# A one-core encoder block: small tiles are widened or added in three pools, so that the tiles behind them begin at multiples of 64 bytes

## The chip, the cores and the metric

The kernel runs on one core of a Trainium2 chip. The metric is the device time of one execution in microseconds (us). Three executions of the kernel before took 2293.75, 2299.6 and 2301.99 us; the median is 2299.6 us.

## The reference

One encoder layer on 2048 positions with 1024 channels, all in float32. Half of the mixer's channels go through a two-dimensional Fourier transform, the other half through a gated long convolution (Hyena) whose filters come from a small network. A squared-ReLU MLP of width 4096 follows.

```python
h   = rmsnorm(x, g_mix);  p = h @ w_in                  # 1024 -> 2048
y_f = rmsnorm(fourier_mix(p[..., :512]), g_fourier)     # Re(FFT2), 8 groups x 64 channels
y_h = rmsnorm(hyena_mix(p[..., 512:], ...), g_hyena)    # z = gate * (fft_long_conv(z, k) + d z), twice
x   = x + concat(y_f, y_h) @ w_out
a   = square(relu(rmsnorm(x, g_mlp) @ w_fc1))           # 1024 -> 4096
x   = x + a @ w_fc2                                     # 4096 -> 1024
out = rmsnorm(x, g_final)
```

## The kernel before

**Two kinds of matmul.** Where float32 accuracy is wanted at speed, an operand is split into a high and a low part of type float32r (`split`, lines 184 to 188: ScalarE casts the high part, VectorE or GpSimd subtracts it for the low part), and `mm3` (lines 198 to 200) issues three matmuls: high by high, high by low, low by high. The transforms use plain float32 matmuls instead, and the trace has two records for each of those. In a matmul the stationary operand is loaded into the array first (LDWEIGHTS) and the moving operand, up to 512 columns, streams past it. A row of the profile such as `p1u<-zf,ahm` names the result, then the moving operand, then the stationary one.

**Stages, in order of time.** `project` (0 to about 410 us) computes `p` in two passes. `filters` (to about 615 us) generates eight spectra: `generate` makes the time-domain filter in two halves `kh` and `kl` (for two of the eight units in one tile `k`), `stage1` multiplies them with the constant table `e1h`, `e1l` by `mm3` in groups of three, `stage2` is plain float32 with the table `f2`. `fourier` runs beside it. `hyena` (to about 840 us) is plain float32: `first` reads `zz`, `second` the table `f2h`, `inverse` the table `a2`, which lies in the tile of `f2`. `project_out` (to about 1040 us) is `mm3` again, then `fc1` (to about 1672 us) and `fc2` (to the end), both with Strassen-like products m1 to m7.

**The MLP's first half.** `fc1` makes 32 steps. A step has seven products (`fc1_product`), each twelve matmuls on one row of 512 tokens: four slices by `mm3`. The moving operands are token tiles that stay: m1 and m2 lie in `zf`, a tile of 32 KB per partition (line 1000); m3, m5, m6 and m7 lie in the tiles `G` and `V` (rows `bm`), m4 in `bhm` and `blm`. The stationary operands are weight slices `ahm` and `alm`, split anew in each step. The order on TensorE within a step is m1 (`p1u<-zf`), m4 of the step before (`p1u<-bhm`), m2 (`p1m<-zf`), m3 of the step before (`p1v<-bm`), m6, m5, m7. After step 15 the token tiles are loaded anew for the second half of the tokens. The last lines of `fc1` make another `zf` in the same place, which holds both operands of the first products of `fc2` (rows `p2u<-zf` and `p2m<-zf`).

**Where a tile lies.** A pool lays its tiles one behind the other in each partition of the on-chip memory, from a left or from a right end; tiles take multiples of 32 bytes. Pools with side "right" (`cp0`, `zp`, `tabs`, `ep`, `norms`, `gk`, `spectra`, `fourier`) are stacked from the high end downwards, and that end lies 32 bytes off a multiple of 64 in this kernel. `uf`, `zz`, `k` (two units) and `zf` are one buffer of `zp` after another. In the built program the tiles that the text speaks of begin at these offsets behind a multiple of 64 bytes:

| tile | before | after | used as |
|---|---|---|---|
| `zf` (fc1) | 32 | 0 | moving, float32r, against `ahm`, `alm` at 0 |
| `zf` (first products of fc2) | 32 | 0 | moving and stationary, float32r |
| `kh`, `kl`, `k` | 32 | 0 | moving, float32r, against `e1h`, `e1l` at 0 |
| `bm`, `bhm`, `blm`, `G`, `V`, `wh`, `xh`, `qah`, `qbh` | 0 | 0 | float32r, both sides |
| `f2`, `f2h`, `emb`, `e1z`, `b1` | 32 | 0 | stationary, float32 |
| `zz`, `uf`, `wo`, `hid`, `feat` | 32 | 0 | moving, float32 |
| `y` | 0 | 0 | moving, float32, against `a2` in the tile of `f2` |
| `ident`, `xt`, `hm` | 0 | 0 | transposes |
| `e1f`, `ones`, `turn` (the table) | 32 | 32 | small constants |

Of the kernel before, what the change touches and what calls it, by code (L numbers as in the profile page):

```python
# [10 lines left out]
F32 = mybir.dt.float32  # L11
# [118 lines left out]
P = 128  # L130
# [6 lines left out]
def hybrid_block(ctx: ExitStack, tc: tile.TileContext, A, out):  # L137
    nc = tc.nc
# [26 lines left out]
    def pool(name, side="left"):  # L165
        return tc.tile_pool(name=name, bufs=1, side=side, reuse_waits="tile")

    def pa(nm):
        return ps.tile([P, 512], F32, tag="a", name=nm, bufs=8)

    def load(pl, tag, shape, src, bufs=1):
        t = pl.tile(shape, F32, tag=tag, name=tag, bufs=bufs)
        nc.sync.dma_start(t, src)
        return t
# [89 lines left out]
    def filter_hidden(fh):  # L264

        yield
        with tc.high_priority(offset=120):
            w0 = load(fh, "w0", [66, P], A["filt_w0"])
            wi = load(fh, "wi", [P, 2, P], A["filt_wi"])
            fb = load(fh, "fb", [P, 4], A["filt_bf"])  # L270
            first = load(fh, "feat", [66, 512], A["feat"][:, 0:512], 2)
        for half in range(2):
            cur = {}
            for layer in range(3):
                for q in (2 * half, 2 * half + 1):
                    if layer == 0:
                        cur[q] = load(fh, "feat", [66, 512], A["feat"][:, 512 * q : 512 * q + 512], 2) if q else first
                    p = pa(f"ph{layer}")
                    nc.tensor.matmul(p, lhsT=w0 if layer == 0 else wi[:, layer - 1, :], rhs=cur[q], start=True, stop=True)
                    a = fh.tile([P, 512], F32, tag="arg", name="arg", bufs=2)  # L280
                    nc.vector.tensor_scalar(out=a, in0=p, scalar1=fb[:, layer : layer + 1], scalar2=fb[:, 3:4], op0=ALU.add, op1=ALU.mult)
                    n = fh.tile([P, 512], F32, tag="turn", name="turn")
                    nc.vector.tensor_scalar(out=n, in0=a, scalar1=1.0 / TAU, scalar2=MAGIC, op0=ALU.mult, op1=ALU.add)
                    nc.vector.tensor_scalar(out=n, in0=n, scalar1=MAGIC, scalar2=None, op0=ALU.subtract)
                    for c in TAU_PARTS:
                        nc.vector.scalar_tensor_tensor(out=a, in0=n, scalar=-c, in1=a, op0=ALU.mult, op1=ALU.add)
                    nc.vector.tensor_scalar(out=a, in0=a, scalar1=PI_IN, scalar2=-PI_IN, op0=ALU.min, op1=ALU.max)
                    if layer < 2:
                        cur[q] = fh.tile([P, 512], F32, tag="hid", name="hid", bufs=2)
                        nc.scalar.activation(cur[q], a, AF.Sin)  # L290
                        yield
                        continue
                    emb = fh.tile([P, 8, P], F32, tag="emb", name="emb", bufs=2)
                    nc.gpsimd.memset(emb, 0.0)
                    for h in (slice(0, 64), slice(64, 128)):
                        nc.scalar.activation(emb[h, :, h], a[h].rearrange("h (l p) -> h l p", l=8), AF.Sin)
                    if q == 0:

                        nc.vector.tensor_copy(emb[64:128, 0, 0:1], emb[0:64, 0, 0:1])
                    nc.sync.dma_start(embd[:, 8 * q : 8 * q + 8, :], emb)  # L300
                    yield
# [207 lines left out]
    def filters(ctx, tp, fx, fp, gp, zp, zzs, norms, emb, wo, e1k, f2, dk8, tabs):  # L509
# [2 lines left out]
        e1h, e1l = (fp.tile([P, P], FR, tag=n, name=n) for n in ("e1h", "e1l"))  # L512
        split(e1h, e1l, e1k)

        longd = fp.tile([P, 8], F32, tag="longd", name="longd")
        p = pa("plongd")
        nc.tensor.transpose(p[:, 0:8], dk8, ident[0:8, 0:8])
        nc.scalar.copy(longd, p[:, 0:8])
# [840 lines left out]
    def run(*steps):  # L1359

        live = list(steps)
        while live:
            live = [g for g in live if next(g, live) is not live]
# [4 lines left out]
    with pool("ip") as ip, pool("cp1") as cp1:  # L1368
        with pool("cp0", "right") as cp0:
            run(project(ip, fx, (cp0, cp1), (1, 2), None), filter_hidden(cp0), fourier_weights(cp0))  # L1370
        zstack, tabs, early = (ctx.enter_context(ExitStack()) for _ in range(3))
        zp = zstack.enter_context(pool("zp", "right"))
        uf = zp.tile([P, NT, 512], F32, tag="zz", name="uf")
        tp = tabs.enter_context(pool("tabs", "right"))
        ep = early.enter_context(pool("ep", "right"))
        got, ffs = [], []

        w2 = A["w_fc2"].rearrange("(h f p) d -> p h f d", h=2, p=P)

        def second_weights(room, tiles):  # L1380


            rows = A["w_fc2"].rearrange("(h f p) d -> p h f d", h=2, p=P)
            room = room.rearrange("p f c -> p (f c)").rearrange("p (n h d) -> p n h d", n=2, h=2)
            for f, tile_f in enumerate(tiles):
                t = room[:, f % 2]
                nc.scalar.copy(t[:, 0, 0:1], uf[:, tile_f, 0:1])
                nc.sync.dma_start(t, rows[:, :, f, :])
                b11, b12, b21, b22 = (t[:, h, 512 * e : 512 * e + 512] for h in range(2) for e in range(2))
                nc.vector.tensor_sub(b11, b12, b11)  # L1390
                nc.vector.tensor_sub(b12, b22, b12)
                nc.vector.tensor_sub(b22, b22, b11)
                nc.vector.tensor_sub(b21, b21, b22)
                nc.sync.dma_start(td[:, f], t.rearrange("p h (e d) -> p (h e) d", e=2))
                yield

        def tables():
            yield
            yield
            got.extend(load(cpool, n, [P, P], A[n]) for n in ("e1f", "e1k", "turn"))  # L1400
            got.append(load(cpool, "gy", [P, 8], A["g_y"]))
            got.append(cpool.tile([8, 128], F32, tag="dk8", name="dk8"))
            for n in range(2):
                nc.sync.dma_start(got[-1][4 * n : 4 * n + 4, :], A["long_d"].rearrange("a (c n) j -> n (a c) j", n=2)[n])
            f2, emb = (pl.tile([P, 32, P], F32, tag=n, name=n) for pl, n in ((tp, "f2"), (tp, "emb")))

            second = second_weights(f2, [15, 0, 0, 1, 2, 3, 4, 5, 6, 7, 8, 9, 10, 11, 12, 13])
            got.append(load(tp, "e1z", [P, 2, P], A["e1z"]))
            got.append(load(ep, "wo", [P, 2, 512], A["filt_wo"]))
            got.extend((emb, f2))  # L1410
            for f in range(0, 32, 8):
                next(second)
                yield
                if f in (0, 8):
                    next(second)
                nc.sync.dma_start(emb[:, f : f + 8], embd[:, f : f + 8])

            for f in (1, 5, 9, 11, 13, 15):
                next(second)
                yield  # L1420
                if f == 1:
                    next(second)
                n = 4 if f < 9 else 2
                t = fx.tile([P, n, 2, P], F32, tag="xt" if n > 2 else "st", name="ff", bufs=6 - n)
                nc.sync.dma_start(t, A["ff"][:, f : f + n])
                ffs.extend(t[:, j : j + 2] for j in range(0, n, 2))
            for _ in second:
                yield
            for f in range(0, 32, 8):
                nc.sync.dma_start(f2[:, f : f + 8], A["f2k"][:, f : f + 8])  # L1430

        run(project(ip, fx, (None, cp1), (-1, 0), uf), tables())
        e1f, e1k, turn, gy, dk8, e1z, wo, emb, f2 = got
    norms = early.enter_context(pool("norms", "right")).tile([P, 4, 128], F32, tag="norms", name="norms")
    with pool("filters") as fp:
        zzs, f2h = [], []
        gp = early.enter_context(pool("gk", "right"))
        spx = early.enter_context(ExitStack())
        filt = filters(spx, tp, fx, fp, gp, zp, zzs, norms, emb, wo, e1k, f2, dk8, f2h)
        with pool("fourier", "right") as fo:  # L1440
            ffs.insert(0, load(fo, "ff0", [P, 1, 2, P], A["ff"][:, 0:1]))
            for i, _ in enumerate(fourier(fo, uf, e1f, ffs)):
                if i % 2 == 0 and i < 16 or 16 <= i < 24:
                    next(filt)
        run(filt)
# [73 lines left out]
```

## Time and profile before

| | |
|---|---|
| three executions | 2293.75, 2299.6, 2301.99 us |
| profiled execution, first to last instruction | 2296.7 us |
| TensorE busy | 2238.5 us, 97% |
| VectorE, ScalarE, GpSimd busy | 65%, 48%, 36% |
| mean granted TensorE clock | 0.991 |
| DMA | 487.31 MB, 212 GB/s over the span |

The profile gives the span of the profiled execution and no separate time for it; the span is 2.9 us under the median of the three executions and within their spread. "Busy" of TensorE counts records whose ends are modelled: matmuls are pipelined, one record of 512 columns lasts 390 ns while the next begins after about 227 ns. So this text reads the distance from start to start in the timeline view (start, length, engine, line, operation, names, shape, count; in brackets idle time before it and what ended that). In the windows view a row has the stretch, its length, and for each engine its busy time and number of records, then the granted clock, the DMA share and GB/s. In the views of one tile or one line, a row has the number of records, the shortest, median and longest duration in ns, and the first and last start.

### The profile page before, as it was taken

Reading aid. Unit: us, or ns where it says so; the run is one execution under the profiler, and the core shown is the slowest. Engines: PE = TensorE matmul, PEld = TensorE weight load, DVE = VectorE, ACT = ScalarE, POOL = GpSimd, SP = SyncE. Lnnn points to the kernel's source line nnn. Section 1 sums busy time; section 2 is a strip of 40 time slices with the busy share of each in tenths; the row PEclk is TensorE's granted clock in tenths of the full one; section 3 lists DMA queues with packets and bytes.
Section 4 is the critical chain, followed back from the end, with each engine's and each line's share of the span. In section 5 each row is a group of like instructions: output and inputs, shape, how many; then the busy total and the mean of one; then the engine's idle time right before and its main releaser. Section 6 shows DMA issues by size and latency. Waiting matters only on the chain.

```text
span 2296.7 us, 31041 instructions
## 1 busy us (share of the span) xinstructions
PE 2238.5 (97%) x11025; PEld 1855.9 (81%) x11025; DVE 1501.3 (65%) x2254; ACT 1108.8 (48%) x1849; POOL 826.0 (36%) x627
## 2 busy tenths in 40 slices
PE   8999999999999989998999989999999999999998
PEld 6887788799788858886888878888888888888886
DVE  6999676777578774458444465444477666866667
ACT  6555211566366564455555565555543333533333
POOL 3444323576476611146555546555400000000000
PEclk9999999999999999999999999999999999999999
DMA  8535886689987766667444475444489766866631
GB/s 270 184 133 198 315 304 247 223 289 324 337 264 210 214 194 188 180 197 234 156 149 150 151 247 164 152 152 151 143 316 344 246 189 196 297 197 194 192 119 74
DMA packets 298798, 487.31 MB, mean 212 GB/s; under 512 B 17478, under 2 KB 141712, under 8 KB 294418
## 3 DMA queue, kind: packets, MB, share of 16 engines
q1 hardware_dynamic: 292977, 470.91, 62.2%
q10 hardware_dynamic: 5664, 14.41, 1.8%
q8 instruction: 87, 1.43, 0.3%
q14 instruction: 70, 0.57, 0.1%
HBM read 314.64 MB, written 169.05 MB: 211 GB/s over the span
## 4 chain that ended last, share of the span: by engine, by line
PE 85%; DVE 5%; DMA 4%; ACT 3%; issue 2%; POOL 1%; SPq 0%; ACTq 0%; DVEq 0%; POOLq 0%
PE p2u L198 5%; PE p2u L199 5%; PE p2u L200 5%; PE p1u L198 5%; PE p1u L200 5%; PE p1u L199 5%; PE pu L200 4%; PE pu L199 4%; PE pu L198 4%; PE p2v L198 3%; PE p2v L199 3%; PE p2v L200 3%; PE pk L610 2%; PE p1v L198 2%; PE p1v L200 2%; PE pz L729 2%
## 5 line engine op out<-in xcount | busy, mean ns | idle before, releaser
L184 ACT CAST qahm<-ra 128x1024 fp32r<-128x1024 f32 x110 | 115.9, 1053 | 345.2 <-PE p2u L199 172.0
L185 DVE TENSOR_TENSOR qalm<-ra,qahm 128x1024 fp32r<-128x1024 f32 x110 | 134.7, 1225 | 153.7 <-ACT qahm L184 151.8
L1293 POOL TENSOR_TENSOR acc<-acc,gfin 128x512 f32<-128x512 f32 x4 | 5.1, 1278 | 631.9 <-DMA out<-acc 624.7
L198 PE MATMUL pu<-wh,xh 128*128 128x512 f32 x512 | 204.3, 400 | 5.6 <-ACT wh L187 4.4
L199 PE MATMUL pu<-wl,xh 128*128 128x512 f32 x512 | 201.7, 394 | 3.7 <-DVE wl L188 3.6
L200 PE MATMUL pu<-wh,xl 128*128 128x512 f32 x512 | 201.6, 394 | 1.2 <-DVE xl L185 1.2
L199 PE MATMUL p2u<-qblm,qahm 128*128 128x512 f32 x504 | 196.3, 390 | 0.0
L198 PE MATMUL p2u<-qbhm,qahm 128*128 128x512 f32 x504 | 196.1, 390 | 0.0
L200 PE MATMUL p2u<-qbhm,qalm 128*128 128x512 f32 x504 | 196.0, 390 | 0.0
L185 DVE TENSOR_TENSOR qblm<-rb,qbhm 128x1024 fp32r<-128x1024 f32 x110 | 134.1, 1219 | 2.6 <-ACT qbhm L184 2.4
L393 POOL TENSOR_TENSOR acc<-acc,cw 128x512 f32<-128x512 f32 x45 | 59.9, 1332 | 196.8 <-DVE acc L370 193.5
L184 ACT CAST ahm<-s 128x512 fp32r<-128x512 f32 x124 | 76.7, 621 | 100.9 <-PE p1v L199 55.3
L185 POOL TENSOR_TENSOR alm<-W,ahm 128x512 fp32r<-128x512 f32 x63 | 86.2, 1369 | 97.8 <-ACT ahm L184 97.8
L198 PEld LDWEIGHTS pu<-wh,xh 128*128 128x128 f32 x512 | 97.2, 190 | 26.3 <-ACT wh L187 4.8
L199 PEld LDWEIGHTS pu<-wl,xh 128*128 128x128 f32 x512 | 97.3, 190 | 25.3 <-DVE wl L188 4.9
L184 ACT CAST qbhm<-rb 128x1024 fp32r<-128x1024 f32 x110 | 115.3, 1048 | 4.7 <-DMA rb<-in_w_fc 3.4
L200 PEld LDWEIGHTS pu<-wh,xl 128*128 128x128 f32 x512 | 97.2, 190 | 22.8 <-DVE xl L185 2.8
L198 PEld LDWEIGHTS p2u<-qbhm,qahm 128*128 128x128 f32 x504 | 94.7, 188 | 20.0 <-issue 0.3
L200 PEld LDWEIGHTS p2u<-qbhm,qalm 128*128 128x128 f32 x504 | 94.7, 188 | 19.6
L199 PEld LDWEIGHTS p2u<-qblm,qahm 128*128 128x128 f32 x504 | 94.7, 188 | 19.5
L198 PE MATMUL p1u<-bm,ahm 128*128 128x512 f32 x252 | 100.3, 398 | 9.4 <-ACT ku L1155 9.4
L184 ACT CAST ahm<-W 128x512 fp32r<-128x512 f32 x94 | 57.5, 615 | 101.5 <-PE p1u L199 101.5
(397 smaller groups left out, 6428.6 us busy)
## 6 DMA issues: line engine op xcount, KB each, us to landing
W<-in_w_fc SPq DMA_DIRECT2D x66, 512.0 KB, 4.6
spec<-ks SPq DMA_DIRECT2D x32, 1024.0 KB, 6.2
ks<-spec SPq DMA_DIRECT2D x64, 512.0 KB, 4.9
rb<-td SPq DMA_DIRECT2D x64, 512.0 KB, 4.1
ra<-a1m SPq DMA_DIRECT2D x56, 512.0 KB, 3.9
ra<-a0m SPq DMA_DIRECT2D x54, 512.0 KB, 5.8
rb<-in_w_fc SPq DMA_DIRECT2D x46, 512.0 KB, 4.9
f<-in_w_fc SPq DMA_DIRECT2D x16, 1024.0 KB, 8.2
```

What stands on the lines that cost most here:

```text
L184: nc.scalar.copy(hi, src)
L185: (eng or nc.vector).tensor_sub(lo, src, hi)
L198: nc.tensor.matmul(o, lhsT=lh, rhs=rh, start=start, stop=False, skip_group_check=more)
L199: nc.tensor.matmul(o, lhsT=lh, rhs=rl, start=False, stop=False, skip_group_check=more)
L200: nc.tensor.matmul(o, lhsT=ll, rhs=rh, start=False, stop=stop, skip_group_check=more)
L393: nc.gpsimd.tensor_add(m1, m1, cw[:, 3, :])
L610: nc.tensor.matmul(p[:, 128 * j : 128 * j + 128], lhsT=f2[:, 4 * q + j, :], rhs=self.G[:, :, 4 * q + j], start=True, stop=True)
L729: nc.tensor.matmul(p[:, 256 * sp : 256 * sp + 256], lhsT=e1[:, sp, :], rhs=zz[:, :, lo : lo + 16], start=True, stop=True)
L1293: nc.gpsimd.tensor_mul(acc[i][:, c], acc[i][:, c], gfin[:, c])
```

## The change

In the pool `cp0` the bias tile `fb` is declared 16 columns wide, of which four are used, and a tile `edge` of 32 bytes is added at the pool's end. In the pool `filters` the tile `longd` is declared 16 columns wide, of which eight are used. In the pool `zp` a tile `edge` of 32 bytes is added beside the large buffer. Nothing reads or writes the added columns or the two `edge` tiles. Each engine gets the same instructions in the same order as before, and TensorE and the DMA queue of SyncE wait for the same events; three instructions elsewhere lose a wait for an earlier DMA, and two such waits of ScalarE move from one instruction (`neg`) to one thirteen instructions later (`sb`). What differs is where tiles lie, by 32 bytes in either direction.

```diff
         with tc.high_priority(offset=120):
             w0 = load(fh, "w0", [66, P], A["filt_w0"])
             wi = load(fh, "wi", [P, 2, P], A["filt_wi"])
-            fb = load(fh, "fb", [P, 4], A["filt_bf"])
+            fb = fh.tile([P, 16], F32, tag="fb", name="fb")[:, 0:4]
+            nc.sync.dma_start(fb, A["filt_bf"])
             first = load(fh, "feat", [66, 512], A["feat"][:, 0:512], 2)
...
-        longd = fp.tile([P, 8], F32, tag="longd", name="longd")
+        longd = fp.tile([P, 16], F32, tag="longd", name="longd")[:, 0:8]
...
             run(project(ip, fx, (cp0, cp1), (1, 2), None), filter_hidden(cp0), fourier_weights(cp0))
+            cp0.tile([P, 8], F32, tag="edge", name="edge")
         zstack, tabs, early = (ctx.enter_context(ExitStack()) for _ in range(3))
         zp = zstack.enter_context(pool("zp", "right"))
         uf = zp.tile([P, NT, 512], F32, tag="zz", name="uf")
+        zp.tile([P, 8], F32, tag="edge", name="edge")
```

## The prediction

> **What bounds the kernel now.** First the head of the page, then the windows view over the stages that the change can reach.
>
> ```profile
> span 2296.7 us, 31041 instructions
> PE 85%; DVE 5%; DMA 4%; ACT 3%; issue 2%; POOL 1%; SPq 0%; ACTq 0%; DVEq 0%; POOLq 0%
> 460.00:575.00 115.00, 115.00 (x870) 106.09 (x869) 88.16 (x158) 72.52 (x147) 81.40 (x69) 1.00 0.87 308
> 1040.00:1080.00 40.00, 35.03 (x149) 28.15 (x150) 31.16 (x32) 26.81 (x45) 24.41 (x15) 0.91 0.80 261
> 1083.00:1351.00 268.00, 268.00 (x1170) 219.41 (x1169) 122.61 (x141) 148.55 (x252) 156.44 (x112) 1.00 0.49 162
> 1378.00:1672.00 294.00, 294.00 (x1271) 240.46 (x1271) 138.51 (x159) 160.64 (x270) 159.94 (x114) 0.99 0.47 152
> 1690.00:2270.00 580.00, 580.00 (x2560) 480.45 (x2559) 404.44 (x491) 231.19 (x252) 0.00 (x0) 1.00 0.66 218
> ```
>
> TensorE holds 85% of the chain that ended last. After the stretch and its length, a window row has TensorE's matmuls, its weight loads, VectorE, ScalarE, GpSimd, granted clock, DMA share and GB/s. In the filters (460 to 575 us), in `fc1` (1083 to 1351 and 1378 to 1672) and in `fc2` TensorE is busy in all of the stretch at a granted clock of 0.99 to 1.00. No other engine passes 77% there, and in `fc1` none passes 60%. So a nanosecond less per matmul in these stretches is a nanosecond less in the span, and the other engines keep up. Only at the start of `fc1` (1040 to 1080) TensorE waits: 35 of 40 us.
>
> Busy time doesn't show whether those matmuls run at full speed. The timeline of one step of `fc1` does. Each row is the first matmul of a run of twelve; the column to read is the start.
>
> ```profile
> 1332.17 0.39 PE L198 MATMUL p1u<-bm,ahm 128*128 128x512 f32 x1
> ...
> 1334.89 0.40 PE L198 MATMUL p1u<-zf,ahm 128*128 128x512 f32 x1
> ...
> 1337.69 0.40 PE L198 MATMUL p1u<-bhm,ahm 128*128 128x512 f32 x1
> ...
> 1340.45 0.40 PE L198 MATMUL p1m<-zf,ahm 128*128 128x512 f32 x1
> ...
> 1343.25 0.40 PE L198 MATMUL p1v<-bm,ahm 128*128 128x512 f32 x1
> ...
> 1346.01 0.39 PE L198 MATMUL p1u<-bm,ahm 128*128 128x512 f32 x1
> ...
> 1348.73 0.39 PE L198 MATMUL p1v<-bm,ahm 128*128 128x512 f32 x1
> ```
>
> Twelve matmuls on `bm` take 2.72 us (1332.17 to 1334.89, and again 1346.01 to 1348.73), which is 227 ns each. Twelve on `zf` take 2.80 us, both times: 233 ns each. And the run behind each `zf` run, though its tile is at offset 0, takes 2.76 us: something that the `zf` run has left behind is worked off there. So a `zf` run costs 0.08 + 0.04 = **0.12 us** more than one on an aligned tile.
>
> Is that the offset? Two more sets of rows bear on it: those of one tile (shortest, median and longest duration in ns, first and last start), and a stretch of the timeline at the start of `fc2`.
>
> ```profile
> L198 PE MATMUL p1u<-zf,ahm x120: 393/397/400, 1080.0 to 1654.9; 128*128 128x512 f32 x120
> L198 PE MATMUL p1v<-bm,ahm x252: 388/390/629, 1068.8 to 1677.8; 128*128 128x512 f32 x126
> L198 PE MATMUL p2m<-zf x8: 389/390/390, 1683.0 to 1687.8; 128*128 128x512 f32 x8
> L198 PE MATMUL pk<-kh,e1h x48: 392/397/496, 456.8 to 604.9; 128*128 128x512 f32 x48
> 1680.55 0.39 PE L199 MATMUL p2u<-zf 128*128 128x512 f32 x1
> ...
> 1683.27 0.39 PE L199 MATMUL p2m<-zf 128*128 128x512 f32 x1
> ```
>
> The median is 397 ns where the moving operand stands at 32 and the stationary one at 0: for `zf` against `ahm`, and also for `kh` against `e1h`, other tiles in another stage. It is 390 ns where both stand at 0 (`bm`), and also where both stand at 32 (`p2m<-zf`): twelve of those take 2.72 us, from 1680.55 to 1683.27. So offset 32 alone costs nothing in a row of like matmuls; a moving operand at 32 beside a stationary one at 0 does. The change sets both to 0, a pair that the trace shows at full speed.
>
> **Part by part: `zf` in `fc1`.** 32 steps with two `zf` runs are 64 runs. The four runs of the first two steps lie between 1040 and 1080 us, where TensorE waits for others anyway; I count them as nothing. The other 60 save 60 x 0.12 = **7.2 us**. Two waits stand in the middle, where the token tiles are loaded anew:
>
> ```profile
> 1354.10 0.50 PE L198 MATMUL p1u<-bm,ahm 128*128 128x512 f32 x1 [2.02 <-ACT ku L1155]
> 1377.59 0.79 PE L198 MATMUL p1u<-bm,ahm 128*128 128x512 f32 x1 [3.82 <-ACT ku L1155]
> 1378.18 0.63 PE L199 MATMUL p1u<-bm,ahm 128*128 128x512 f32 x1
> ...
> 1382.87 0.63 PE L199 MATMUL p1u<-zf,ahm 128*128 128x512 f32 x1
> ```
>
> The loads and splits behind them start from TensorE's last use of the old tiles, which comes earlier by what was saved until then, so they keep that saving; within a step TensorE arrives up to 0.24 us sooner, so at most some 0.2 us are given back at each. After the longer wait eleven matmuls take 4.69 us (1378.18 to 1382.87), 426 ns each instead of 227: the array runs at half its rate for that long. [...] I take nothing for it; twelve matmuls at 0.2 us more, 2.4 us, are a bound upwards, well inside the range below.
>
> **`kh`, `kl`, `k` in the filters.** 192 matmuls stand at 32 against 0, but in short runs between plain float32 work. What does an aligned run look like there? `project_out` shows one behind transposes:
>
> ```profile
> 482.02 0.40 PE L199 MATMUL pk<-k,e1h 128*128 128x512 f32 x1
> ...
> 483.19 0.38 PE L542 MATMUL pk<-wo,emb 128*128 128x128 f32 x2
> 562.48 0.40 PE L199 MATMUL pk<-kl,e1h 128*128 128x512 f32 x1
> ...
> 567.85 0.83 PE L542 MATMUL pk<-wo,emb 128*128 128x128 f32 x6
> 899.81 0.40 PE L199 MATMUL po<-G,oyh 128*128 128x512 f32 x1
> ...
> 900.97 0.39 PE L198 MATMUL po<-V,oyh 128*128 128x512 f32 x1
> ...
> 902.35 0.39 PE L198 MATMUL po<-G,oyh 128*128 128x512 f32 x1
> ```
>
> Counted from the second matmul, a run of six takes 1.17 us in the filters (482.02 to 483.19) and its first five take 1.16 us in `project_out` (899.81 to 900.97): aligned runs start slowly too, so a short one gains 0.01 us, and one of twelve not much more. A run of 24 takes 5.37 us (562.48 to 567.85) against 2.54 us for eleven aligned (899.81 to 902.35) and 12 x 0.227 = 2.72 us for the rest, 5.26 us: 0.11 us. There are two runs of 24 and 19 shorter ones: 0.22 + 19 x 0.015 = **0.5 us**.
>
> **The plain float32 matmuls.** The tables `f2`, `f2h`, `a2` and `emb` come from 32 to 0, in 4 x 512 = 2048 records.
>
> ```profile
> L752 PE MATMUL pv<-y,f x512: 270/275/579, 633.1 to 820.3; 128*128 128x128 f32 x171
> L542 PE MATMUL pk<-wo,emb x512: 270/275/418, 408.3 to 583.5; 128*128 128x128 f32 x171
> L610 PE MATMUL pk<-Gk,f x512: 269/273/379, 466.6 to 613.7; 128*128 128x128 f32 x171
> L736 PE MATMUL pz<-G,f2h x512: 270/273/422, 621.7 to 812.0; 128*128 128x128 f32 x171
> L233 PE MATMUL pt_m<-ident,hm x128: 272/273/330, 860.7 to 1047.4; 128*128 128x128 f32 x128
> ```
>
> With the stationary table at 32, the moving operand at 0 (`y`) and at 32 (`wo`) have the same median, 275 ns: here the pair's offsets don't matter. The trace has no such matmul with both at 0; the nearest are the transposes, at 273 ns. So between a gain of 2 ns and, by the same distance the other way, a loss of 2 ns: 2048 x 2 = 4.1 us either side. I take 0, by the two equal rows. The wider tiles, the `edge` tiles and the five moved waits add no work to any engine.
>
> **Sum.** 7.2 + 0.5 = 7.7 us off a span of 2296.7 us gives 2289.0 us. The median of the executions is 2.9 us over that span, so 2299.6 - 7.7 = **2291.9 us**, -0.33%. A measurement of this kernel can tell about 0.5% (11.5 us) from no change, so the forecast lies inside that.
>
> **Rivals.** (1) *The change does nothing*: 2299.6 us. Offset 32 is not what slows the `zf` runs; it is something else about their place. For it: `p2m<-zf` in the same bytes runs at 390 ns. Against it: `kh` shows the same 397 ns elsewhere, and the pair of offsets tells all these rows apart. [...] (2) *The float32 matmuls gain too*: 2291.9 - 4.1 = 2287.8 us, if both operands at 0 give what the transposes show. (3) *The other side: float32 matmuls with both at 0 get slower*, because moving and stationary reads that start alike collide. From 7.7 us / 2048 = 3.8 ns a record on the gain is gone; at the 7 ns that `zf` shows (397 against 390) they would cost 14.3 us: 2299.6 + 6.6 = 2306.2 us. Against it: float32r pairs at 0 and 0 are the fastest rows there are, and the rows of lines 542 and 752 do not react to the moving operand's offset.
>
> **How the numbers follow.** Forecast 72%, rival 1 15%, rival 2 8%, rival 3 5%. The three executions before spread over 8 us, so a median of a few can be 3 us off. The range goes from rival 2's 2287.8 less 3 to rival 1's 2299.6 and half a microsecond: 2285 to 2300, which leaves out rival 3 and the noisy half of rival 1. Faster by over 0.5% needs 2288.1 or less: most of rival 2 and a tenth of the forecast, 0.15. Slower by over 0.5% needs 2311: 0.03, rival 3 at a higher price. Within: 0.82.
>
> **What the changed profile would show.** Right: the `zf` rows at a median of 390 ns, 2.72 us from run to run through the whole step, a step of `fc1` of 84 x 0.2267 = 19.04 us instead of 19.28; `pk<-kh` runs of 24 at 5.26 us; lines 542, 610, 736 and 752 at 273 to 275 ns. Rival 1: `zf` stays at 397. Rivals 2 and 3: lines 542 and 752 move. Wrong altogether: the waits before 1354 and 1377 us grow by what was saved.

## Result and profile after

Five executions of the kernel after took 2286.55 to 2289.84 us, median **2289.36 us**. Five of the kernel before have a median of 2298.18 us. The ratio is 0.9963, with a 95% interval of 0.9952 to 0.9974: faster by 0.4%, 8.8 us.

The head of the page:

```profile
span 2288.0 us, 31038 instructions
PE 2229.5 (97%) x11025; PEld 1854.2 (81%) x11025; DVE 1503.7 (66%) x2254; ACT 1109.5 (48%) x1849; POOL 827.4 (36%) x627
```

Two rows of the windows view (stretch, length, then TensorE, weight loads, VectorE, ScalarE and GpSimd, granted clock, DMA share, GB/s):

```profile
460.00:575.00 115.00, 115.00 (x870) 106.36 (x869) 88.87 (x159) 72.21 (x146) 82.26 (x69) 1.00 0.87 307
1690.00:2270.00 580.00, 580.00 (x2559) 479.73 (x2558) 405.27 (x502) 230.44 (x253) 0.00 (x0) 1.00 0.64 215
```

The span is 8.7 us shorter, and TensorE is as busy as before, 97% of the span and all of these stretches, at the same clock. The shares alone show no change. The timeline of a step of `fc1` does (first matmul of each run of twelve; the column to read is the start):

```profile
1327.89 0.39 PE L198 MATMUL p1u<-bm,ahm 128*128 128x512 f32 x1
...
1330.61 0.39 PE L198 MATMUL p1u<-zf,ahm 128*128 128x512 f32 x1
...
1333.33 0.39 PE L198 MATMUL p1u<-bhm,ahm 128*128 128x512 f32 x1
...
1336.05 0.39 PE L198 MATMUL p1m<-zf,ahm 128*128 128x512 f32 x1
...
1338.77 0.39 PE L198 MATMUL p1v<-bm,ahm 128*128 128x512 f32 x1
```

Every run now takes 2.72 us, whichever tile moves. The runs on `zf` took 2.80 us before, and the runs behind them 2.76 us. How much that adds up to is read from the rows of one tile: `p1m<-zf` of `fc1`, before and then after (shortest, median and longest duration in ns, first and last start).

```profile
L198 PE MATMUL p1m<-zf,ahm x120: 394/397/400, 1089.8 to 1660.4; 128*128 128x512 f32 x120
```

```profile
L198 PE MATMUL p1m<-zf,ahm x120: 389/389/389, 1088.5 to 1651.9; 128*128 128x512 f32 x120
L198 PE MATMUL pk<-kh,e1h x48: 387/394/501, 457.6 to 605.1; 128*128 128x512 f32 x48
L737 PE MATMUL pz<-G,f2h x512: 270/272/421, 621.9 to 811.2; 128*128 128x128 f32 x171
L753 PE MATMUL pv<-y,f x512: 270/275/550, 633.8 to 820.3; 128*128 128x128 f32 x171
L543 PE MATMUL pk<-wo,emb x512: 269/275/422, 407.5 to 583.7; 128*128 128x128 f32 x171
```

The kernel after is 1.3 us ahead at the first of these matmuls (1089.8 against 1088.5) and 8.5 us ahead at the last (1660.4 against 1651.9). So `fc1` gave 7.2 us of the 8.7. In the filters the first `kh` matmul starts 0.8 us later than before and the last 0.2 us later: 0.6 us were won there. The rows of plain float32 stand where they stood: 275 ns for lines 543 and 753, 272 instead of 273 for line 737. What is left, about 0.9 us, came from waits elsewhere: by the start times the kernel after loses 0.8 us ahead of the filters, gains 1.5 us between the filters and `fc1`, and 0.2 us behind it. Such waits differ from execution to execution: the eight kernels below that are the same as the kernel after up to `fc1` reach their first `kh` matmul anywhere between 455.6 and 461.5 us.

### The profile page after: what moved, and what is told of

Same layout as the page of the kernel before. It is cut to its first block, busy times and chain, and to the rows that moved or that the text cites. A ratio compares the mean times of both kernels' runs of the same rounds, so it can differ in the third digit from the quotient of the medians.

```text
span 2288.0 us, 31038 instructions
## 1 busy us (share of the span) xinstructions
PE 2229.5 (97%) x11025; PEld 1854.2 (81%) x11025; DVE 1503.7 (66%) x2254; ACT 1109.5 (48%) x1849; POOL 827.4 (36%) x627
## 4 chain that ended last, share of the span: by engine, by line
PE 81%; DVE 3%; DMA 2%; ACT 2%; issue 1%; POOL 1%; SPq 0%; ACTq 0%; POOLq 0%; DVEq 0%
PE p2u L198 5%; PE p2u L199 5%; PE p2u L200 5%; PE p1u L200 5%; PE p1u L198 5%; PE p1u L199 5%; PE p2v L198 3%; PE p2v L199 3%; PE p2v L200 3%; PE pv L753 2%; PE pu L200 2%; PE pu L199 2%; PE pu L198 2%; PE pk L611 2%; PE p1v L200 2%; PE p1v L199 2%
```

## Experiments

The expectations name their theories themselves; theory A is the reason that the prediction gives, that the pair of offsets modulo 64 decides. All diffs are against the kernel after, unless the text says otherwise. A median of several executions comes with a ratio and its interval; where there is one execution, no ratio is given.

**One line of the change alone.** Of the whole change only the `edge` tile of the pool `zp` is kept:

```diff
         uf = zp.tile([P, NT, 512], F32, tag="zz", name="uf")
+        zp.tile([P, 8], F32, tag="edge", name="edge")
```

> Only the 32-byte tile in the pool of zf is added; kh and kl of four units stay at 32, and so does what lies in cp0. Theory A (a matmul is slow where its moving and its stationary row begin at different offsets mod 64) and theory B (a moving row that begins at 32 is slow, whatever the stationary one does): zf rows go to 389 ns, fc1 gains the 7.4 us that it gained with the whole change, the filters some 0.2 us; 0.9966 of before, 2290 to 2291 us. Theory C (the place of zf or the shift of the left pools does it, not the offset mod 64): no more than half of that.

Measured: 2289.8 us, ratio 0.9963 (0.9950 to 0.9975), the same as the whole change.

```profile
L198 PE MATMUL p1m<-zf,ahm x120: 389/389/389, 1088.3 to 1651.3; 128*128 128x512 f32 x120
L198 PE MATMUL pk<-kh,e1h x48: 389/397/483, 456.7 to 604.0; 128*128 128x512 f32 x48
```

`zf` is at 389 ns, and from its first to its last row here `fc1` takes 563.0 us, where the kernel before takes 570.6: 7.6 us. So the place of `zf` is nearly the whole gain, and the other three edits can't be seen in the total. The line moves more than `zf`, though: all pools stacked behind `zp` on the right side shift with it, and so `k` and some `kh` tiles come to their new place too. The `kh` rows stay at 397 in the median, with the tiles of the left pool still in their old place.

**The filters' line alone.** Only `longd` is widened:

```diff
-        longd = fp.tile([P, 8], F32, tag="longd", name="longd")
+        longd = fp.tile([P, 16], F32, tag="longd", name="longd")[:, 0:8]
```

> Only longd is widened: kh and kl of three or four units in the left pool come to 0, zf stays at 32. Theories A and B: zf rows stay at 397 ns, fc1 as before; runs of kh in the filters lose 0.01 us each, the one run of 24 that is moved 0.1 us; the time is that of before within 0.5 us of its usual scatter. Theory C: part of the gain of fc1 shows here.

Measured: 2297.61 us in one execution, beside a median of 2297.3 for the kernel before. Twelve matmuls on `zf` still take 2.80 us, and the twelve behind them 2.76:

```profile
1296.13 0.40 PE L198 MATMUL p1u<-zf,ahm 128*128 128x512 f32 x1
...
1298.93 0.40 PE L198 MATMUL p1u<-bhm,ahm 128*128 128x512 f32 x1
...
1301.69 0.40 PE L198 MATMUL p1m<-zf,ahm 128*128 128x512 f32 x1
```

**Is it the place of `zf`, or the pair?** The weight rows `ahm`, `alm` are moved 32 bytes on (m1 and m2 of the first two steps, and m5 and m6 of the first, take their weights from another pool and stay):

```diff
+        mp.tile([P, 8], F32, tag="pad0", name="pad0")
         for h in "hl":
             mp.tile([P, 4, P], FR, tag=f"a{h}", name=f"a{h}", bufs=9)
+        mp.tile([P, 8], F32, tag="pad1", name="pad1")
```

> The kernel after, with the stationary weights of fc1 moved to 32 by a 32-byte tile in front of them (steps 2 to 31; another behind them keeps the rest in place). Every pair in fc1 is then 0 against 32. Theory A: all 84 matmuls of a step are slow, 233 to 237 ns each instead of 227, a step takes 19.6 to 19.9 us instead of 19.04, and the kernel 2306 to 2315 us. Theories B and C: nothing moves, 2289 us, since no moving row has changed.

Measured: 2305.93 us, ratio 1.0037 (1.0026 to 1.0048). Slower than the kernel *before*: now every run takes 2.80 us, though `zf`, `G` and `V` lie where the kernel after has them (`bhm` and `blm` begin 64 bytes further on).

```profile
1300.55 0.40 PE L198 MATMUL p1u<-zf,ahm 128*128 128x512 f32 x1
...
1303.35 0.40 PE L198 MATMUL p1u<-bhm,ahm 128*128 128x512 f32 x1
...
1320.14 0.40 PE L198 MATMUL p1u<-zf,ahm 128*128 128x512 f32 x1
```

A step takes 19.6 us (1300.55 to 1320.14) instead of 19.04, and the total is at the low end of what theory A expected. So it is no property of the moving tile alone. The next kernel also takes the `edge` tile of `zp` away, so that `zf` and the weights are both 32 bytes off:

```diff
-        zp.tile([P, 8], F32, tag="edge", name="edge")
```

> As e3, and zf at 32 too (its pool's small tile is left out). m1 and m2 then pair 32 with 32, the other five products 0 with 32. Theory A: the zf runs are the fast ones (2.72 us) and the other 60 matmuls of a step slow: 12 to 18 us over the kernel after, 2301 to 2308 us. Theory B: the zf runs are slow and nothing else, 2297 us as before. Theory C: as before, 2297 us.

Measured: 2305.15 us, ratio 1.0036 (1.0024 to 1.0047).

```profile
1300.25 0.39 PE L198 MATMUL p1u<-zf,ahm 128*128 128x512 f32 x1
...
1302.99 0.40 PE L198 MATMUL p1u<-bhm,ahm 128*128 128x512 f32 x1
...
1305.80 0.40 PE L198 MATMUL p1m<-zf,ahm 128*128 128x512 f32 x1
...
1308.56 0.40 PE L198 MATMUL p1v<-bm,ahm 128*128 128x512 f32 x1
```

Now the twelve on `zf` take least (2.74 and 2.76 us), and all others 2.80 us. The two `zf` runs don't reach 2.72 because the first five and seven of their matmuls are still spaced more widely; the rest go at 227 ns. The place of one operand relative to the other counts, and theory A holds up to here.

**How far off must a tile be?** Four kernels begin the tile `bhm` of m4 4, 16, 32 or 64 bytes further on. Each of the two tiles is also made 64 bytes longer, so `blm`, which lies behind `bhm`, begins 64 bytes further on than that: 68, 80, 96 or 128. All else stays. Of the twelve matmuls of a run eight move `bhm` and four `blm`, so each run mixes two distances. The kernel for 32 bytes:

```diff
-        b["m4"] = [mp.tile([P, 4, 512], FR, tag=f"b{h}m4", name=f"b{h}m4") for h in "hl"]
+        b["m4"] = [mp.tile([P, 2048 + 16], FR, tag=f"b{h}m4", name=f"b{h}m4")[:, 8 : 8 + 2048].rearrange("p (k f) -> p k f", k=4) for h in "hl"]
```

> The kernel after, with the token tiles of m4 (bhm, blm: another pool, far from zf) begun 32 bytes later. Theory A (pair of offsets mod 64): the bhm run costs 2.80 us instead of 2.72 and the run behind it 0.04 us more; 32 runs, 3.8 us on the kernel after. Theory C (only the place of zf): nothing changes.

> The same with 16 bytes. If a row is read in lines of 64 bytes, one that begins at 16 touches 33 lines as one at 32 does: the same 2.80 + 0.04 us. If lines of 16 bytes (or of 32 with two halves) matter, 16 costs less than 32 or nothing.

> The same with 4 bytes. Lines of 64 bytes: again 33 lines, 2.80 + 0.04 us. Lines of 16 bytes: this is the only offset of the four that should cost anything.

> The same with 64 bytes: the tile has moved as in the others, and its offset mod 64 is 0 again. Theory A: 2.72 us, the kernel after. If moving the tile as such matters, this one shows it.

One execution each, beside 2298.67 us for the kernel before. Medians over the runs of `bhm` and over the `zf` runs (`p1m`) behind them, worked out from the start times (bytes are those of `bhm`):

| bytes | us | `bhm` run, ns | run behind, ns |
|---|---|---|---|
| 0 (kernel after) | 2289.36 | 2720 | 2720 |
| 4 | 2294.68 | 2843 | 2730 |
| 16 | 2292.22 | 2763 | 2770 |
| 32 | 2295.79 | 2788 | 2719 |
| 64 | 2293.00 | 2792 | 2749 |

The last row breaks theory A as it was worded. At 64 bytes every tile again begins at a multiple of 64, and yet the run takes 2792 ns. Nor does either rule of lines in the expectations give this order: 4 bytes cost most (2843 ns) and 16 least (2763 ns). In the timeline of the kernel for 64 bytes, the `bhm` run takes 2.79 us and the `zf` run behind it 2.75:

```profile
1296.46 0.40 PE L198 MATMUL p1u<-bhm,ahm 128*128 128x512 f32 x1
...
1299.25 0.39 PE L198 MATMUL p1m<-zf,ahm 128*128 128x512 f32 x1
...
1302.00 0.39 PE L198 MATMUL p1v<-bm,ahm 128*128 128x512 f32 x1
```

**The distance between the two rows, in one kernel.** The weights of `fc1` pass through nine buffers in turn. If each buffer is a little longer than its tile, the nine lie at nine different distances from every moving tile, and one execution measures all of them. First in steps of 64 bytes:

```diff
+        ROOM = (16, 16, 16, 16, 16, 16, 16, 16, 0)
...
+            t = mp.tile([P, 512 + ROOM[s]], FR, tag=f"a{h}{s}", name=f"a{h}{n}")
...
-                a[n] = [mp.tile([P, 4, P], FR, tag=f"a{h}", name=f"a{h}{n}", bufs=9) for h in "hl"]
+                a[n] = [slot(h, n) for h in "hl"]
```

> The kernel after; the nine weight slots of fc1 lie 0, 64, 128, 192, 256, 320, 384, 448 and 512 bytes further on than before, the moving rows stay. m4_off64 was slow although 64 is 0 mod 64, so theory A as worded (mod 64) has fallen or that run had another cause. Theory D: what counts is the distance between the start of the moving row and of the stationary row, with a longer period. Period 512: all slots but 0 and 512 are slow by 4 to 8 ns a matmul, 9 to 16 us on the kernel after. Period 128: the slots 0, 128, 256, 384 and 512 are at 227 ns, the four others slow, 5 to 9 us. Period 64 (theory A, m4_off64 then due to the absolute place of its rows): all slots at 227 ns, the time of the kernel after.

and then in steps of 16 bytes:

> The same with slots at 0, 16, 32, 48, 64, 80, 96, 112 and 128. Theory D: slot 0 at 227 ns, 32 at 233 ns as in e3_weights32, 64 as slow as or slower than 227 by 3 to 8 ns; 128 at 227 ns only if the period is 128. Whether the cost falls off steadily with the distance or comes in steps shows here. A distance at which a matmul comes below 227 ns would be new: nothing in the traces so far shows one.

One execution each: 2303.29 and 2301.07 us, beside 2296.47 for the kernel before. Four runs behind each other in the first of the two kernels, by the start of their first matmul; the weights of the first three lie in the buffers at 0, 64 and 256 bytes:

```profile
1296.34 0.39 PE L198 MATMUL p1v<-bm,ahm 128*128 128x512 f32 x1
...
1299.06 0.40 PE L198 MATMUL p1u<-bm,ahm 128*128 128x512 f32 x1
...
1301.85 0.39 PE L198 MATMUL p1u<-zf,ahm 128*128 128x512 f32 x1
...
1304.60 0.39 PE L198 MATMUL p1u<-bhm,ahm 128*128 128x512 f32 x1
```

They take 2.72, 2.79 and 2.75 us; the third loses its 0.03 us in its first matmuls, which follow the twelve of 2.79 us. To leave such starts out: for each run of twelve, the mean distance from start to start of its eighth to eleventh matmul, grouped by how far the stationary row begins behind the moving row in the built program (modulo 512 bytes; some 24 runs each, twice as many at 0 of the left half):

| steps of 64: bytes | ns | steps of 16: bytes | ns |
|---|---|---|---|
| 0 | 226.7 | 0 | 227.2 |
| 64 | 233.3 | 16 | 230.7 |
| 128 | 233.8 | 32 | 233.2 |
| 192 | 230.3 | 48 | 233.3 |
| **256** | **226.7** | 64 | 233.4 |
| 320 | 233.3 | 80 | 232.7 |
| 384 | 232.8 | 96 | 234.5 |
| 448 | 230.0 | 112 | 233.4 |

The left half repeats after 256 bytes; of the periods named beforehand (512, 128, 64) none came out. So a second theory takes A's place: a stream of float32r matmuls goes at 226.7 ns where the starts of its two rows differ by a multiple of **256** bytes, and is slower on average at every other distance measured, by 3 to 8 ns. The means hide some order. At 16 bytes no run lies near the mean: ten of 25 go at 226.5 to 226.8 ns, all ten directly behind a run at 0 or 128 bytes, and the others at 233.0 to 233.8. At 192 and 448 single runs lie at 228 to 230 or at 233. By the same addresses `zf` of the kernel before lies at 224 modulo 256, and in the kernel after at 0.

**The new theory against "multiples of 64".** Two kernels shift the weights as above, by 64 and by 256 bytes (first pad 16 or 64 columns; the second pad returns `bhm` to its place modulo 256). The second kernel also declares `longd` 64 columns wide, which brings `kh` and `kl` of the filters' left part from a distance of 192 to 0.

```diff
+        mp.tile([P, 16], F32, tag="pad0", name="pad0")
         for h in "hl":
             mp.tile([P, 4, P], FR, tag=f"a{h}", name=f"a{h}", bufs=9)
+        mp.tile([P, 48], F32, tag="pad1", name="pad1")
```

> Edit: the kernel after, with the weight rows of fc1 64 bytes further on in every step but the first two, so that every large tile of fc1 begins at a multiple of 64 bytes, and zf, bhm and the weights of one matmul stand 64 bytes apart modulo 256. Theory 'distance modulo 256' (a float32r matmul goes at 226.7 ns only where the starts of its moving and its stationary row differ by a multiple of 256 bytes): every run of twelve in fc1 at 2.80 us instead of 2.72, one step 19.60 us instead of 19.04, in all about 30 steps x 0.56 = 16.8 us above the kernel after: 2304 to 2308 us, as the kernel with the weights 32 bytes on gave (2305.9). Rival 'multiples of 64' (it is enough that both rows begin at multiples of 64): runs of 2.72 us, 2288 to 2291 us.

> Edit: the kernel after, with the weight rows of fc1 256 bytes further on in every step but the first two, and longd widened to 64 columns, by which the tiles behind it in the left pool move on and kh, kl of the filters' left part come to a distance of 0 modulo 256 from their stationary rows (before: 192). Theory 'distance modulo 256': fc1 as in the kernel after, runs of 2.72 us, step 19.04 us; the left part's kh and kl runs of six at or below 1.15 us, a gain of 0.1 us at most; in all 2287.5 to 2291 us, within 0.3 per cent of the kernel after. Rival 'any shift of the weights costs' (what the shifted weights brought was the shift of other tiles behind them, or another place in the memory, and not the distance): 2300 us or more, runs of 2.75 us or above. Rival 'multiples of 64': 2288 to 2291 us here as well as in the kernel with the weights 64 bytes on.

Measured with 64 bytes: 2304.83 us, ratio 1.0032 (1.0019 to 1.0045), a step of 19.60 us:

```profile
1300.39 0.39 PE L198 MATMUL p1u<-zf,ahm 128*128 128x512 f32 x1
...
1303.19 0.39 PE L198 MATMUL p1u<-bhm,ahm 128*128 128x512 f32 x1
...
1319.99 0.39 PE L198 MATMUL p1u<-zf,ahm 128*128 128x512 f32 x1
```

With 256 bytes: 2292.28 us, ratio 0.9974 (0.9964 to 0.9983), a step of 19.04 us:

```profile
1295.22 0.39 PE L198 MATMUL p1u<-zf,ahm 128*128 128x512 f32 x1
...
1297.94 0.39 PE L198 MATMUL p1u<-bhm,ahm 128*128 128x512 f32 x1
...
1314.26 0.39 PE L198 MATMUL p1u<-zf,ahm 128*128 128x512 f32 x1
```

and its rows of `p1m<-zf`:

```profile
L198 PE MATMUL p1m<-zf,ahm x120: 389/389/389, 1091.2 to 1654.8; 128*128 128x512 f32 x120
```

A kernel in which every large tile of `fc1` begins at a multiple of 64 bytes is slower than the kernel before, and a shift by 256 leaves every run at 2.72 us. "Multiples of 64" and "any shift costs" fall; the distance modulo 256 stands. The total of the second kernel misses the expected range by 1.3 us and lies 2.9 us above the kernel after. That isn't `fc1`: its `p1m<-zf` rows begin 2.7 us later than in the kernel after (1091.2 against 1088.5) and end 2.9 us later. The difference is there before `fc1` is in its stride. Whether the wider `longd` makes it stays open. One profile can't tell: this one reaches the first `zf` matmul of `p1m` at 1044.4 us, the kernel after and the eight others with its `longd` and the same work up to there between 1042.3 and 1046.8. But the ten executions here (2290.69 to 2293.33 us) and the five of the kernel after (2286.55 to 2289.84), taken at another time, don't overlap.

The filters, another stage with other tiles, agree with the same theory. From the second matmul of a run of six to the plain float32 work behind it, by the start times: 1.168 us where `kh`, `k` lie at 224 modulo 256 (kernel before), 1.157 us at 192 (kernel after, left part), 1.145 us at 0 (kernel after, right part; with `longd` at 64 columns both parts).

## Why the prediction was right

The forecast was 2291.9 us in a range of 2285 to 2300, "within 0.5%"; the time is 2289.36 us, 0.4% faster. That range held "no change" too, so the total alone proves little; the rows of the parts do. The terms were right, the reason behind them only in part, and one wait went another way.

**`zf` in `fc1`.** Forecast 7.2 us (60 runs at 0.12 us); the `p1m<-zf` rows show 7.2 us. The parts of the 0.12 us are there too: a `zf` run went from 2.80 to 2.72 us and the run behind it from 2.76 to 2.72, so that a step lasts 19.04 us as forecast. The kernel with the `edge` tile of `zp` alone shows that this is the cause, and not something else in the change.

**`kh`, `kl`, `k`.** Forecast 0.5 us; the `kh` rows show 0.6, and the lengths of all 21 runs from their second matmul on, summed from the start times, differ by 0.51 us. The size of one part was off: of the two runs of 24 only one gained, and more than forecast:

```profile
562.90 0.40 PE L199 MATMUL pk<-kl,e1h 128*128 128x512 f32 x1
...
568.13 1.05 PE L543 MATMUL pk<-wo,emb 128*128 128x128 f32 x8
```

It takes 5.23 us (before 5.37, forecast 5.26). The other, with stalls inside, took 7.21 us before and after.

**Plain float32.** Forecast 0 within 4.1 us either way. The rows don't move, and by the start times of the same matmuls the kernel after goes from 0.6 to 0.9 us ahead between 658 and 834 us: 0.3 us over nearly all of `hyena`. Rivals 2 and 3, a gain or a loss there, fall for this change. What a distance of 0 modulo 256 would do to these matmuls no run shows, since their distances were not worked out.

**Rival 1, "the change does nothing"**, falls with 389 ns for `zf`. Nor is it the place of `zf` alone: moving the stationary rows alone, by 32 or by 64 bytes, slowed every run from 2.72 to 2.80 us.

**The reason.** The prediction said that a moving operand at 32 beside a stationary one at 0 (modulo 64) is slow, and that "the change sets both to 0, a pair that the trace shows at full speed". The trace of before could not tell 64 from 256: the pairs that the prediction read at 227 ns were at a distance of 0 modulo 256, those at 233 ns at 224. The change itself is worded by multiples of 64 too, and that its 32 bytes bring `zf` to 0 modulo 256 as well was luck. For `kh` and `kl` of the left part they don't (192), and those gained only half.

**The two waits in the middle.** The prediction took nothing for matmuls at half rate behind them. No run shows that zero: the runs showed 1.6 us given back at the first wait, with matmuls at half rate behind it. Before, then after (timeline; in brackets the wait):

```profile
1351.45 0.40 PE L198 MATMUL p1u<-zf,ahm 128*128 128x512 f32 x1
...
1362.03 0.40 PE L198 MATMUL p1m<-zf,ahm 128*128 128x512 f32 x1
...
1388.42 0.40 PE L198 MATMUL p1m<-zf,ahm 128*128 128x512 f32 x1
```

```profile
1346.93 0.39 PE L198 MATMUL p1u<-zf,ahm 128*128 128x512 f32 x1
...
1349.66 0.50 PE L198 MATMUL p1u<-bm,ahm 128*128 128x512 f32 x1 [2.11 <-ACT ku L1156]
...
1352.26 0.63 PE L200 MATMUL p1u<-bm,alm 128*128 128x512 f32 x1
...
1352.69 0.63 PE L198 MATMUL p1u<-bm,ahm 128*128 128x512 f32 x1
...
1359.12 0.39 PE L198 MATMUL p1m<-zf,ahm 128*128 128x512 f32 x1
...
1373.57 0.50 PE L198 MATMUL p1u<-bm,ahm 128*128 128x512 f32 x1 [3.18 <-ACT ku L1156]
...
1383.26 0.39 PE L198 MATMUL p1m<-zf,ahm 128*128 128x512 f32 x1
```

The wait grew from 2.02 to 2.11 us only, and yet matmuls behind it go at half rate (records of 0.63 us). The windows view with TensorE alone (stretch, length, busy time and records, granted clock, DMA share, GB/s) shows what differs. First two stretches of the kernel before, then two of the kernel after:

```profile
1349.24:1352.66 3.42, 2.84 (x13) 1.00 1.00 340
1352.66:1356.07 3.41, 1.97 (x9) 1.00 0.52 202
```

```profile
1347.43:1350.84 3.41, 1.30 (x6) 1.00 0.51 199
1350.84:1354.26 3.42, 3.42 (x10) 0.50 1.00 336
```

The stretches are steps of 3.41 us; within each execution every change of the granted clock lies on such a grid; in these two traces, between 20 and 2270 us it stays at half for 3.41 or 6.83 us each time. Before, the wait was split over two steps, 0.58 and 1.44 us idle; after, its 2.11 us lie in one step, and the next step is granted half the clock. So in these runs the place of the wait on the grid decided, and not its length: with both at 32 a longer one (2.69 us from start to start) lay across two steps and was followed by no matmul at 427 ns, and with `longd` alone a shorter one (2.36 us) lay in one step and was followed by seven. At the rows of the timeline above, the kernel after is 4.52 us ahead at the first row (1351.45 against 1346.93) and 2.91 us at the second (1362.03 against 1359.12): 1.6 us given back. The second wait is shorter than before (3.18 against 3.82 us) and has fewer matmuls at half rate behind it (seven at 427 ns from start to start, against twelve), and at 1388.42 against 1383.26 the lead is 5.16 us. Over both the account closes, so the total didn't show the error; the bound of 2.4 us that the prediction set held.

**The level.** The time is 2.5 us under the forecast: 1.1 us because the median fell by 8.8 instead of 7.7 us, and 1.4 us because the forecast started from the median of three executions, 2299.6 us, where five have 2298.18. The 2.9 us that it carried over from span to median came from that scatter: every execution on record with both figures is 1.75 to 1.93 us longer than its own span.

## What to carry to other kernels

When TensorE is busy without a gap, read the distance from start to start of like matmuls, not their busy time: 6.7 ns of 227 showed no trace in any share. For streams of float32r matmuls like those of `fc1`, place the moving and the stationary tile at the same offset modulo 256 bytes: a step took 19.04 us so. Rounding each to 64 was not enough (19.60 us), and moving one operand alone by 32 bytes made the whole stage slower (19.6 us). Test an alignment rule by breaking it on the other operand: one pad of 32 bytes separated "this tile" from "this pair", and nine buffers at nine distances gave the period in one execution. Where a short wait may cost clock, look at the granted clock in the steps around it, and not at the wait's length alone: a wait of 2.02 us was followed by no matmul at half rate here, and one of 2.11 us by seven.

## What the runs showed of the hardware

- A stream of float32r matmuls of 512 columns is spaced by 226.7 ns at a distance of 0 modulo 256 bytes between its two rows and by 230 to 234.5 ns on average at the other distances measured (16 to 224 in the two kernels with nine distances); the run that mixes 4 and 68 bytes took 237 ns a matmul (2843 ns for twelve). At 16 bytes ten of 25 runs kept 226.7 ns. Why, no run here shows. Nor do the runs tell whether a matmul's own stationary row counts or the one that is loaded for the next matmul (in the kernel after, a load of 0.19 us begins at 1327.89 us with one matmul, and the matmul that uses it at 1328.12): within a run both lie at the same distance.
- In these runs the spacing followed a change of distance late. Of twelve matmuls at distance 0 behind twelve at another, the first seven were spaced more widely in the kernel before, and none to ten in the kernels with m4 moved (2719 to 2770 ns for the run); so up to 0.05 us is lost. This is the 0.04 us that the prediction had read as worked off behind `zf`.
- In the fourteen traces the granted clock changed in steps of 3.41 us. Between 20 and 2270 us a step at full clock was followed by one at half 85 times, and in each of these TensorE had stood idle for 1.81 us or more, by its records; in none of the steps at full clock that were followed by another was it idle for more than 1.86. In the kernel before and the kernel after alone there were 13 such times, with 1.97 us or more, and 1.66 at most in the others. Around 1350 us a wait was split over two steps in the kernel before and with both at 32 (2.41 and 2.69 us from start to start, no matmul at 427 ns), and lay in one step in the kernel after and with `longd` alone (2.50 and 2.36 us, seven matmuls at 427 ns instead of 227, 1.4 us).
